# Delta-rule layer: a head's log decays as eight lines in device memory, spread onto a stored mask by an adding transfer

## The chip, the cores and the metric

The kernel runs on one core of one Trainium2 chip, as one launch. The metric is the device time of an execution in microseconds; a kernel's time is the median over its runs. Six units matter here: TensorE (PE, matrix products, with its weight loads as PEld), VectorE (DVE), ScalarE (ACT), GpSimd (POOL), the sync engine (SP, which only issues transfers), and the DMA engines. Each engine works through its own list of instructions in the order laid down when the kernel is built, and waits on semaphores for what others produce.

## What is computed

A bidirectional encoder trunk of two residual layers over 512 tokens of width 1024. Layer 0 mixes the tokens with a gated delta rule, layer 1 with gated linear attention; each is followed by a layer norm, a squared-ReLU feed-forward part and another layer norm. The change lies in layer 0, whose core is, for each of 8 heads and for both directions of time:

```
gc = cumsum(g.reshape(bn, h, n, CHUNK), axis=-1)              # log decays
decay_mat = exp(where(causal, gc[..., :, None] - gc[..., None, :], -inf))
a_mat = where(strict, (kb @ k.T) * decay_mat, 0.0)
sol = triangular_solve(a_mat + I, concat([v * beta, kb * exp(gc)]))
qk = (q @ k.T) * decay_mat
q_dec = q * exp(gc)
for each chunk:                                               # scan
    v_new = u - w @ state
    o = q_dec @ state + qk @ v_new
    state = state * exp(gc_last) + k_dec.T @ v_new
```

Queries and keys are normalized to unit length first. The backward direction is the same on flipped time, and both outputs are added.

## The kernel before

The kernel is written in Python; its loops are unrolled, a scheduler lays out every engine's instructions from the order of the program (earlier lines first, as far as their inputs and buffers are estimated to be free), and allocates buffers from pools by tag. It takes chunks of 128 tokens, so NT = 4 chunks per direction, and 8 chunk problems per head. All products of the projections are made from a high and a low half in three passes (`mm3`, L128 to L130).

`gdn` (L1337) runs the heads as a pipeline written out by hand. In round i it traces `recur` of head i-2 (the scan over chunks), `solve` of head i-1 (the triangular solve by doubling) and `project` of head i (four projections of 512 columns: k, q, v, z, each with a five-tap convolution), then `finish` of head i-2. The scheduler interleaves them, so the projections of one head and, after the last head, the output products (`oa`, the rows of `out_pieces`) stand between the dependent steps of the others.

The steps that the change touches, for head h:

- `GdnConst.masks` (L1170) builds constants on POOL in the setup: a bf16 identity `idb`, a selector `sel` of 6 x 2 x 128 (tag "E" while it is built), two bf16 triangles `mi` holding 0 or -1e30, and masks that the change leaves alone.
- `rows` (L1463), run after the q projection of head h has been convolved and passed through Silu. It squares and sums the transposed k and q, takes logarithms, and forms at L1488 the row sums `rw`: for every token and direction the cumulated log decay less half the logarithm of the key's squared norm. L1490 to L1496 split `rw` into three bf16 parts on DVE; L1499 turns them by four bf16 transposes into the bank `rtp`; L1501 copies the 6 x 512 result to `rt` on ACT. `cj` (L1502) holds the other side's terms per token.
- `solve` (L1519). `kk` (L1528) are the products of the keys. L1532 to L1539: for each direction a matmul with `sel` spreads the rows over all partitions in a PSUM bank `ep` (L1534), its exponential times q gives the query factors `qd` (L1536, L1537). L1547 to L1549 add the triangle to the same bank by a matmul with `idb`. L1553 takes exponentials of the bank, one per chunk, with `cj` as bias, into `E`. `E` times the masked `kk` (L1555) becomes the matrix `ath`, `atl`, from which the inverse is built: `hp` (L1569), `xp` and the copy `Xd` (L1585, L1587), `lv` (L1614) with `pz`, `Dd` and `Xd` in five sizes, and `nw` (L1660, L1661, L1682). L1674 multiplies `E` with the products of keys and queries into `qke`.
- `recur` (L1687): products `m` (L1708) with `vd`, `vn`, `r`, `sn`, then `op` (L1744), the only reader of `qd`.
- `load_z` (L1351) takes a buffer of tag "qd" for one tile of the residual after the last head.

The banks in PSUM are ch 2, pj 3, tp 1, ac 2: `rtp`, `kk` and the transposes of k, q, v use the single bank of tp; `ep`, `hp`, `xp`, `lv`, `nw`, `qk` share the two of ac. Buffers: `E` two tiles of 2 KB per partition (one direction each), `qd` four. `ath`, `atl`, `a4`, `Dd`, `Xd` have one buffer each, so the solves of two heads can't overlap from `ath` on. Weights come through SP into three buffers `wst`, are cast by ACT to `wh` (L102) and completed by DVE as `wl` (L107). Until the layer norm's parameters are fetched after the heads, POOL has only the setup's masks to make. ACT's function tables are changed around each Silu (L1453 and L57).

Of the kernel before, what the change touches and what calls it, by code (L numbers as in the profile page):

```python
# [17 lines left out]
P = 128  # L18
# [1103 lines left out]
class GdnConst:  # L1122


    def __init__(self, c, pool, w_in, w_g, a_log, dt_bias, conv_w, norm_g, x):
        self.c, self.pool = c, pool
        nc = c.nc
        G, V = nc.gpsimd, nc.vector

        M = 4 * A_H  # L1130
        st = c.wst.tile([P, KT, M], F32, name="bst", tag="wst")
        k0 = c.wst.tile([P, KT, P], F32, name="wst", tag="wst")
        c.new_xt()
        c.new_x()

        c.dma(c.xt[0], x[0])
        c.dma(k0, w_in[A_H])
        c.dma(st, w_g)
# [12 lines left out]
        self.ones = pool.tile([P, P], F32, name="ones", tag="vn", bufs=9)  # L1151
        V.memset(self.ones, 1.0)

        self.pz = {}
        for s in (4, 8, 16, 32, 64):
            self.pz[s] = pool.tile([P, 2 * NT, P], F16, name=f"pz{s}", bufs=1)
            V.memset(self.pz[s], 0.0)
        self.gates(st, k0, bia, coef, cw)
        self.ng = pool.tile([P, 1], F32, name="ng", bufs=1)
        nc.sync.dma_start(self.ng, norm_g.unsqueeze(1), allow_slow_non_contiguous=True)  # L1160
        self.masks()
# [8 lines left out]
    def masks(self):  # L1170
        c, pool = self.c, self.pool
        G = c.nc.gpsimd
        self.idb = pool.tile([P, P], BF16, name="idb", bufs=1)
        G.tensor_copy(self.idb, c.ident)
        self.idh = pool.tile([P, P], F16, name="idh", bufs=1)
        G.tensor_copy(self.idh, c.ident)

        sf = pool.tile([6, 2, P], F32, name="self", tag="E", bufs=2)
        G.memset(sf, 0.0)
        for s in range(3):  # L1180
            G.affine_select(out=sf, in_=sf, compare_op=ALU.not_equal, fill=1.0, base=-2 * s,
                            pattern=[[-1, 2], [0, P]], channel_multiplier=1)
        self.sel = pool.tile([6, 2, P], BF16, name="sel", bufs=1)
        G.tensor_copy(self.sel, sf)
        self.mi = [pool.tile([P, P], BF16, name=f"mi{d}", bufs=1) for d in range(2)]
        for d in range(2):
            t = pool.tile([P, P], F32, name="tri", tag="cf", bufs=2)
            self.tri(t, d, False, 0.0, NEG)
            G.tensor_copy(self.mi[d], t)

        self.nd = pool.tile([P, P], F32, name="nd", bufs=1)
        G.tensor_scalar(self.nd, c.ident, -1.0, 1.0, ALU.mult, ALU.add)

        self.same4 = pool.tile([P, P], F16, name="same4", bufs=1)
        self.off = {}
        prev = None
        for w in (4, 8, 16, 32):
            f = pool.tile([P, P], F32, name="blk", tag="cf", bufs=2)
            G.memset(f, 1.0)
            fv = f.rearrange("p (a b) -> p a b", b=w)  # L1200
            G.affine_select(out=fv, in_=fv, compare_op=ALU.is_ge, fill=0.0, base=0,
                            pattern=[[-w, P // w], [0, w]], channel_multiplier=1)
            G.affine_select(out=fv, in_=fv, compare_op=ALU.is_ge, fill=0.0, base=w - 1,
                            pattern=[[w, P // w], [0, w]], channel_multiplier=-1)
            if w == 4:
                G.tensor_copy(self.same4, f)
            else:
                m = pool.tile([P, NT, P], F16, name=f"off{w // 2}", bufs=1)
                G.tensor_tensor(m, f.unsqueeze(1).to_broadcast([P, NT, P]), prev.unsqueeze(1).to_broadcast([P, NT, P]),
                                ALU.subtract)  # L1210
                self.off[w // 2] = m
            prev = f

        ic = pool.tile([P, P // 4, 4], F32, name="ic", tag="cf", bufs=2)
        G.tensor_copy(ic, c.ident.rearrange("p (b c) -> p b c", c=4))
        n = P // 4
        while n > 1:
            n //= 2
            G.tensor_tensor(ic[:, :n, :], ic[:, :n, :], ic[:, n:2 * n, :], ALU.add)
        self.ic = pool.tile([P, 4], F16, name="icc", bufs=1)  # L1220
        G.tensor_copy(self.ic, ic[:, 0, :])
# [115 lines left out]
def gdn(c, w_in, conv_w, a_log, dt_bias, norm_g, w_out, ln_g, ln_b, x, xt, w_next):  # L1337
    tc, nc = c.tc, c.nc
    w_in, w_g = w_in
    with c.banks(ch=2, pj=3, tp=1, ac=2), tc.tile_pool(name="gdn", bufs=1) as pool:  # L1340
        g = GdnConst(c, pool, w_in, w_g, a_log, dt_bias, conv_w, norm_g, xt)
        hi = [c.big.tile([P, 2, S], F32R, name=f"oh{t}", tag=f"xt{t}") for t in range(NT)]
        lo = [pool.tile([P, 2, S], F32R, name="ol", tag="ol", bufs=NT) for t in range(NT)]
        heads = [GdnHead(c, pool, g, h, w_in, hi[h // 2][:, h % 2, :], lo[h // 2][:, h % 2, :]) for h in range(A_H)]
# [6 lines left out]
        def load_z(hf):  # L1351
            if hf:
                tl = pool.tile([P, NT, S], F32, name="z", tag="sil", bufs=3)
            else:
                tl = heads[-1].next.kq
                more = [heads[-1].t2(tag, n).rearrange("p n i -> p (n i)") for tag, n in (("kt", 3), ("qd", 4))]
            for t in range(NT):
                z[t][hf] = tl[:, t, :] if hf or t < 2 else more[t - 2]
                c.dma(z[t][hf], x[t * P:(t + 1) * P, 512 * hf:512 * hf + 512])
# [27 lines left out]
class GdnHead:  # L1387
# [35 lines left out]
    def project(self, done):  # L1423
# [6 lines left out]
        for i, ci in enumerate((A_H + h, h, 2 * A_H + h, 3 * A_H + h)):  # L1430
# [22 lines left out]
                c.exp_ln_after(A.activation(t, t, AF.Silu))  # L1453
            yield 0.69, 0.0
            if i == 1:
                rows = self.rows(done)
                if h:
                    yield from rows
                else:
                    next(rows)  # L1460
                    next(rows)

    def rows(self, done):  # L1463
# [18 lines left out]

        rw = c.small.tile([P, NT, 2], F32, name="rw", tag="rw")
        self.cj = cj = c.small.tile([P, NT, 2], F32, name="cj", tag="cj")
        lnk = lnr[:, 0, :].unsqueeze(2).to_broadcast([P, NT, 2])
        V.scalar_tensor_tensor(rw, lnk, -0.5, g.gc[:, :, :, h], ALU.mult, ALU.add)  # L1488

        rs = c.small.tile([P, NT, 6], BF16, name="rsp", tag="rsp")  # L1490
        r1 = c.small.tile([P, NT, 2], F32, name="r1", tag="r1")
        V.tensor_copy(rs[:, :, 0:2], rw)
        V.tensor_tensor(r1, rw, rs[:, :, 0:2], ALU.subtract)
        V.tensor_copy(rs[:, :, 2:4], r1)
        V.tensor_tensor(r1, r1, rs[:, :, 2:4], ALU.subtract)
        V.tensor_copy(rs[:, :, 4:6], r1)  # L1496
        rtp = self.bank("rtp", BF16, tag="tp")
        for n in range(NT):
            T.transpose(rtp[:6, n, :], rs[:, n, :], g.idb)  # L1499
        self.rt = pool.tile([6, S], BF16, name="rt", tag="rt", bufs=2)  # L1500
        A.copy(self.rt, rtp[:6, :, :].rearrange("p n i -> p (n i)"))  # L1501
        V.scalar_tensor_tensor(cj, lnk, -0.5, g.lg[:, :, :, h], ALU.mult, ALU.add)  # L1502

        pos = c.small.tile([P, NT, 2], F32, name="neg", tag="neg")
# [14 lines left out]
    def solve(self, done):  # L1519
# [8 lines left out]
            T.matmul(kk[:, n, :], self.kc(n), self.kc(n), start=True, stop=True)  # L1528
        yield 0.9, 0.3

        eps, self.qd = [], []
        for d in range(2):  # L1532
            ps = self.bank("ep")
            T.matmul(ps, g.sel[:, d, :], self.rt, start=True, stop=True)  # L1534
            x = self.t2("qd", 4)
            A.activation(x, ps, AF.Exp)  # L1536
            V.tensor_tensor(x, self.kq[:, 1, :].rearrange("p (n i) -> p n i", n=NT), x, ALU.mult)  # L1537
            self.qd.append(x)
            eps.append(ps)  # L1539
        yield 0.63, 1.4  # L1540

        ath, atl = t8("ath", 1), t8("atl", 1)
        kks = self.t2("on", 2)
        V.tensor_tensor(kks, kk, g.nd.unsqueeze(1).to_broadcast([P, NT, P]), ALU.mult)
        a4 = t8("a4", 1)
        ex, ats = [], []
        with c.in_order(mybir.EngineType.PE):  # L1547
            for d in (1, 0):
                T.matmul(eps[d], g.idb, g.mi[d].unsqueeze(1).to_broadcast([P, NT, P]), start=False, stop=True, skip_group_check=True)  # L1549
        for d, ps in enumerate(eps):  # L1550
            e = self.t2("E", 2)
            for n in range(NT):
                A.activation(e[:, n, :], ps[:, n, :], AF.Exp, bias=self.cj[:, n, d:d + 1])  # L1553
            at = kks if d else self.t2("on", 2)
            V.tensor_tensor(at, e, kks, ALU.mult)  # L1555
            us = slice(d * NT, (d + 1) * NT)
# [28 lines left out]
            T.transpose(xp[:, u, :], dd[:, u, :], g.idh)  # L1585
        xd = t8("Xd", 1)
        A.copy(xd, xp)  # L1587

        def half(t, s, i):

# [96 lines left out]
    def recur(self, done):  # L1687
# [51 lines left out]
        self.op = op = self.bank("op", tag="ch")  # L1739
        for n in (1, 2, 0, 3):  # L1740
            mm = [(self.qke[d][:, n, :], vns[d][n]) for d in range(2)]
            mm += [(self.qd[d][:, n, :], states[d][n]) for d in range(2) if states[d][n] is not None]
            for i, (l, r) in enumerate(mm):
                T.matmul(op[:, n, :], l, r, start=i == 0, stop=i == len(mm) - 1)  # L1744
            if n == 2:
# [100 lines left out]
```

## Time and profile before

| | |
|---|---|
| median of 3 runs | 1327.92 us (1327.11 to 1327.92) |
| the profiled execution | 1328.52 us, of which the span from first to last instruction is 1326.6 |
| granted TensorE clock, mean | 0.997 |
| instructions | 22309 |
| DMA | 154.36 MB, 116 GB/s in the mean |
| layer 0's heads, first row sums to last output products | about 42 to 394 us |

The profile has a page (busy shares, 40 slices, queues, the chain of work that ended last, the costliest groups) and views that can be asked for a stretch of time, an engine, a tile or a line of the program. A timeline row reads: start, length, engine, line, operation, tile written <- tiles read, shape, count, and in brackets how long the engine had been idle and what released it. Lengths of matmuls overlap, because they are pipelined, so the time that one takes from PE is read from the distance between starts. A group row reads: line, engine, operation, tiles, count, and the minimum, median and maximum length in ns. A DMA row gives the size and the median time from issue to landing. PE's operations have a line of the helper that issued them, where there is one.

### The profile page before, as it was taken

The page shows a single profiled execution, that of the slowest core. Times are in us where ns is not written, and L with a number is a line of the kernel's source. Part 1 is how long each engine was busy: PE and PEld are TensorE (multiplying, and loading weights), DVE is VectorE, ACT ScalarE, POOL GpSimd, SP SyncE. Part 2 cuts the span into 40 slices and gives each one's busy share as a digit, 9 for nine tenths or more (in the row PEclk, how much of TensorE's full clock was granted, in tenths as well). Part 3 has the DMA queues.
Part 4 walks back from the last instruction along what each step waited for, and adds up shares of the span by engine and source line. Part 5 has one row for each costly group of instructions (what it writes and reads, how often), then busy time and mean ns, then how long its engine had stood idle before and what let it go on. Part 6 is the DMA issues. An engine that isn't in the chain of part 4 may idle for free.

```text
span 1326.6 us, 22309 instructions
## 1 busy us (share of the span) xinstructions
PE 1307.4 (99%) x8659; PEld 1113.2 (84%) x8659; DVE 1107.7 (83%) x1823; ACT 805.2 (61%) x1598; POOL 124.8 (9%) x177
## 2 busy tenths in 40 slices
PE   9999999999999999999999999999999999999996
PEld 7777877787777889999998888888889889999985
DVE  7787888888668988989988787967879789989887
ACT  4757666767643666566667754654456466666656
POOL 5000000000000910101102200000001001101021
PEclk9999999999999999999999999999999999999998
DMA  5210120211222585675648521111216465657465
GB/s 181 96 49 33 49 65 33 64 49 57 73 99 85 189 178 154 156 191 153 151 150 170 149 90 64 65 63 64 95 64 213 105 193 154 149 172 161 142 143 143
DMA packets 44045, 154.36 MB, mean 116 GB/s; under 512 B 5419, under 2 KB 5795, under 8 KB 43939
## 3 DMA queue, kind: packets, MB, share of 16 engines
q1 hardware_dynamic: 32163, 110.85, 24.9%
q0 software_dynamic: 11776, 42.08, 16.1%
q8 instruction: 68, 1.11, 0.3%
q14 instruction: 38, 0.31, 0.1%
HBM read 113.99 MB, written 2.10 MB: 88 GB/s over the span
## 4 chain that ended last, share of the span: by engine, by line
PE 92%; ACT 3%; DVE 3%; issue 1%; DVEq 0%; POOL 0%; ACTq 0%; POOLq 0%
PE fx L128 3%; PE fx L130 3%; PE fx L129 3%; PE pX L130 3%; PE pX L129 3%; PE pX L128 3%; PE pjv L128 3%; PE pjv L129 3%; PE pjv L130 3%; PE m L1708 3%; PE fyz L128 3%; PE fyz L129 3%; PE fyz L130 3%; PE pY L129 2%; PE pY L128 2%; PE pY L130 2%
## 5 line engine op out<-in xcount | busy, mean ns | idle before, releaser
L102 ACT CAST wh<-wst 128x1024 fp32r<-128x1024 f32 x152 | 159.4, 1049 | 110.3 <-PE fyz L129 35.3
L107 DVE TENSOR_TENSOR wl<-wst,wh 128x1024 fp32r<-128x1024 f32 x150 | 184.3, 1229 | 42.2 <-ACT wh L102 41.9
L107 DVE TENSOR_TENSOR w2l<-w2r,w2h 128x1024 fp32r<-128x1024 f32 x92 | 112.3, 1221 | 24.0 <-ACT w2h L102 23.8
L102 ACT CAST w2h<-w2r 128x1024 fp32r<-128x1024 f32 x94 | 98.5, 1048 | 47.4 <-PE pX L130 16.2
L415 POOL DMA_DIRECT2D w2r<-w2r x56 | 48.5, 892 | 493.9 <-DVE w2l L107 247.3
L102 ACT CAST ah<-h 128x1024 fp32r<-128x1024 f32 x56 | 58.9, 1052 | 40.8 <-PE pX L129 18.1
L464 DVE TENSOR_TENSOR wst<-wst 128x512 f32<-128x512 f32 x120 | 79.8, 685 | 0.4
L107 DVE TENSOR_TENSOR al<-h,ah 128x1024 fp32r<-128x1024 f32 x56 | 68.3, 1220 | 5.1 <-ACT ah L102 4.8
L130 PE MATMUL pX<-w2h,al 128*128 128x512 f32 x168 | 66.2, 394 | 0.0
L129 PE MATMUL pX<-w2l,ah 128*128 128x512 f32 x168 | 66.1, 393 | 0.0
L128 PE MATMUL pX<-w2h,ah 128*128 128x512 f32 x168 | 65.8, 392 | 0.0
L128 PE MATMUL pjv<-wh,xth 128*128 128x512 f32 x128 | 54.7, 427 | 0.0
L128 PE MATMUL fx<-xth,wh 128*128 128x256 f32 x192 | 53.6, 279 | 0.0
L130 PE MATMUL fx<-xh,wl 128*128 128x256 f32 x192 | 53.6, 279 | 0.0
L130 PE MATMUL fyz<-xh,wl 128*128 128x256 f32 x192 | 53.6, 279 | 0.0
L128 PE MATMUL fyz<-xh,wh 128*128 128x256 f32 x192 | 53.6, 279 | 0.0
L128 PE MATMUL fx<-xh,wh 128*128 128x256 f32 x192 | 53.5, 278 | 0.0
L129 PE MATMUL fx<-xl,wh 128*128 128x256 f32 x192 | 53.5, 278 | 0.0
L130 PE MATMUL fx<-xth,wl 128*128 128x256 f32 x192 | 53.4, 278 | 0.0
L129 PE MATMUL fx<-xtl,wh 128*128 128x256 f32 x192 | 53.4, 278 | 0.0
L129 PE MATMUL fyz<-xl,wh 128*128 128x256 f32 x192 | 53.4, 278 | 0.0
L129 PE MATMUL pj<-xtl,wh 128*128 128x256 f32 (+1 forms) x160 | 52.0, 326 | 0.2 <-DVE xtl L194 0.2
(538 smaller groups left out, 4320.7 us busy)
## 6 DMA issues: line engine op xcount, KB each, us to landing
wst<-in_w SPq DMA_DIRECT2D x68, 512.0 KB, 4.3
w2r<-in_w SPq DMA_DIRECT2D x60, 512.0 KB, 4.0
w2r<-w2r POOLq DMA_DIRECT2D x56, 512.0 KB, 5.3
wst<-in_a_in SPq DMA_DIRECT2D x32, 512.0 KB, 3.3
wst<-in_b_vr SPq DMA_DIRECT2D x16, 512.0 KB, 3.3
wst<-in_a_out SPq DMA_DIRECT2D x8, 512.0 KB, 3.3
wst<-in_b_in SPq DMA_DIRECT2D x8, 512.0 KB, 3.3
wst<-in_b_out SPq DMA_DIRECT2D x8, 512.0 KB, 3.3
```

Of the source, the lines that this page charges most:

```text
L102: h = nc.scalar.copy(hi, src)
L107: self.halves = h, nc.vector.tensor_tensor(lo, src, hi.bitcast(F32), ALU.subtract)
L128: mm(ps, ah, bh, start=start, stop=False, **kw)
L129: mm(ps, ah, bl, start=False, stop=False, **kw)
L130: self.last_mm = mm(ps, al, bh, start=False, stop=stop, **kw)
L415: nc.gpsimd.dma_start(blocks[a + (q,)], blocks[b + (q,)], accum_op=ALU.add)
L464: plus = lambda a, b: V.tensor_tensor(a, a, b, ALU.add)
L1708: T.matmul(ps[:, d, :], *ops(d), start=True, stop=True)
```

## The change

The row sums are kept in f32 and turned by one transpose into eight lines of 128 (two directions, four chunks). ACT copies them to SBUF and writes them to a tile in device memory. Two transfers from POOL spread these 4 KB over the 128 partitions: one adds them onto a tile `E` that a transfer from SP has filled with the triangles (0 or -1e30, stored once in device memory by the setup), the other writes them plainly to `qd`. The exponentials of `E` then work in place in SBUF, with the same bias as before. The query factors are made from `qd` in place, further down in `solve`, behind the copy of `Xd`. The split, the selector, the bf16 identity, the bf16 triangles and the four matmuls into `ep` are gone. `E` is now one tile for both directions with two buffers of 4 KB per partition, `qd` likewise.

```diff
 def masks(self):
-        self.idb = pool.tile([P, P], BF16, name="idb", bufs=1)
-        G.tensor_copy(self.idb, c.ident)
...
-        sf = pool.tile([6, 2, P], F32, name="self", tag="E", bufs=2)
...
-        self.sel = pool.tile([6, 2, P], BF16, name="sel", bufs=1)
-        G.tensor_copy(self.sel, sf)
-        self.mi = [pool.tile([P, P], BF16, name=f"mi{d}", bufs=1) for d in range(2)]
+        later = pool.tile([P, 2, P], F32, name="later", bufs=1)
         for d in range(2):
-            t = pool.tile([P, P], F32, name="tri", tag="cf", bufs=2)
-            self.tri(t, d, False, 0.0, NEG)
-            G.tensor_copy(self.mi[d], t)
+            self.tri(later[:, d, :], d, False, 0.0, NEG)
+        self.later = self.dram.tile([P, 2, NT, P], F32, name="laterd", bufs=1)
+        for n in range(NT):
+            G.dma_start(self.later[:, :, n, :], later)
...
 def load_z(hf):
-                more = [heads[-1].t2(tag, n).rearrange("p n i -> p (n i)") for tag, n in (("kt", 3), ("qd", 4))]
+                more = [heads[-1].t2("kt", 3).rearrange("p n i -> p (n i)"),
+                        pool.tile([P, 2, S], F32, name="qd", tag="qd", bufs=2)[:, 0, :]]
...
 def project(self, done):
             if i == 1:
+                self.e = pool.tile([P, 2, NT, P], F32, name="E", tag="E", bufs=2)
+                c.nc.sync.dma_start(self.e, g.later)
                 rows = self.rows(done)
...
 def rows(self, done):
-        rw = c.small.tile([P, NT, 2], F32, name="rw", tag="rw")
+        rdn = c.small.tile([P, 2, NT], F32, name="rw", tag="rw")
+        rw = rdn.rearrange("p d n -> p n d")
...
-        V.tensor_copy(rs[:, :, 0:2], rw)
-        V.tensor_tensor(r1, rw, rs[:, :, 0:2], ALU.subtract)
-        V.tensor_copy(rs[:, :, 2:4], r1)
-        V.tensor_tensor(r1, r1, rs[:, :, 2:4], ALU.subtract)
-        V.tensor_copy(rs[:, :, 4:6], r1)
-        rtp = self.bank("rtp", BF16, tag="tp")
-        for n in range(NT):
-            T.transpose(rtp[:6, n, :], rs[:, n, :], g.idb)
-        self.rt = pool.tile([6, S], BF16, name="rt", tag="rt", bufs=2)
-        A.copy(self.rt, rtp[:6, :, :].rearrange("p n i -> p (n i)"))
+        rtp = self.bank("rtp", shape=(2 * NT, P), tag="tp")
+        T.transpose(rtp, rdn.rearrange("p d n -> p (d n)"), c.ident)
+        rt = pool.tile([2 * NT, P], F32, name="rt", tag="rt", bufs=2)
+        A.copy(rt, rtp)
+        row = g.dram.tile([2 * NT, P], F32, name="row", tag="row", bufs=3)
+        self.qd = pool.tile([P, 2, NT, P], F32, name="qd", tag="qd", bufs=2)
+        c.nc.scalar.dma_start(row, rt)
+        every = row.rearrange("u p -> (u p)").partition_broadcast(P)
+        c.nc.gpsimd.dma_start(self.e.rearrange("p d n i -> p (d n i)"), every, accum_op=ALU.add)
+        c.nc.gpsimd.dma_start(self.qd.rearrange("p d n i -> p (d n i)"), every)
...
 def solve(self, done):
-        eps, self.qd = [], []
-        for d in range(2):
-            ps = self.bank("ep")
-            T.matmul(ps, g.sel[:, d, :], self.rt, start=True, stop=True)
-            x = self.t2("qd", 4)
-            A.activation(x, ps, AF.Exp)
-            V.tensor_tensor(x, self.kq[:, 1, :].rearrange("p (n i) -> p n i", n=NT), x, ALU.mult)
-            self.qd.append(x)
-            eps.append(ps)
-        yield 0.63, 1.4
...
-        with c.in_order(mybir.EngineType.PE):
-            for d in (1, 0):
-                T.matmul(eps[d], g.idb, g.mi[d].unsqueeze(1).to_broadcast([P, NT, P]), start=False, stop=True, skip_group_check=True)
-        for d, ps in enumerate(eps):
-            e = self.t2("E", 2)
+        for d in range(2):
+            e = self.e[:, d, :, :]
             for n in range(NT):
-                A.activation(e[:, n, :], ps[:, n, :], AF.Exp, bias=self.cj[:, n, d:d + 1])
+                A.activation(e[:, n, :], e[:, n, :], AF.Exp, bias=self.cj[:, n, d:d + 1])
...
         A.copy(xd, xp)
+        for d in range(2):
+            x = self.qd[:, d, :, :]
+            A.activation(x, x, AF.Exp)
+            V.tensor_tensor(x, self.kq[:, 1, :].rearrange("p (n i) -> p n i", n=NT), x, ALU.mult)
```

`recur` reads `self.qd[:, d, n, :]` in place of `self.qd[d][:, n, :]`, and `GdnConst` is given the pool in device memory.

More of the change, by code (lines that the diff above doesn't have):

```diff
@@ L1122, with __init__ @@
 class GdnConst:
-    def __init__(self, c, pool, w_in, w_g, a_log, dt_bias, conv_w, norm_g, x):
-        self.c, self.pool = c, pool
+    def __init__(self, c, pool, dram, w_in, w_g, a_log, dt_bias, conv_w, norm_g, x):
+        self.c, self.pool, self.dram = c, pool, dram
         nc = c.nc
@@ L1172, in masks @@
         G = c.nc.gpsimd
-        self.idb = pool.tile([P, P], BF16, name="idb", bufs=1)
-        G.tensor_copy(self.idb, c.ident)
         self.idh = pool.tile([P, P], F16, name="idh", bufs=1)
         G.tensor_copy(self.idh, c.ident)
-        sf = pool.tile([6, 2, P], F32, name="self", tag="E", bufs=2)
[L1179 to L1182, printed above, removed]
-        self.sel = pool.tile([6, 2, P], BF16, name="sel", bufs=1)
-        G.tensor_copy(self.sel, sf)
-        self.mi = [pool.tile([P, P], BF16, name=f"mi{d}", bufs=1) for d in range(2)]
+        later = pool.tile([P, 2, P], F32, name="later", bufs=1)
         for d in range(2):
-            t = pool.tile([P, P], F32, name="tri", tag="cf", bufs=2)
-            self.tri(t, d, False, 0.0, NEG)
-            G.tensor_copy(self.mi[d], t)
+            self.tri(later[:, d, :], d, False, 0.0, NEG)
+        self.later = self.dram.tile([P, 2, NT, P], F32, name="laterd", bufs=1)
+        for n in range(NT):
+            G.dma_start(self.later[:, :, n, :], later)
         self.nd = pool.tile([P, P], F32, name="nd", bufs=1)
@@ L1339, in gdn @@
     w_in, w_g = w_in
-    with c.banks(ch=2, pj=3, tp=1, ac=2), tc.tile_pool(name="gdn", bufs=1) as pool:
-        g = GdnConst(c, pool, w_in, w_g, a_log, dt_bias, conv_w, norm_g, xt)
+    with c.banks(ch=2, pj=3, tp=1, ac=2), tc.tile_pool(name="gdn", bufs=1) as pool, \
+            tc.tile_pool(name="gdr", bufs=1, space=bass.MemoryType.DRAM) as dram:
+        g = GdnConst(c, pool, dram, w_in, w_g, a_log, dt_bias, conv_w, norm_g, xt)
         hi = [c.big.tile([P, 2, S], F32R, name=f"oh{t}", tag=f"xt{t}") for t in range(NT)]
@@ L1488, in rows @@
         V.scalar_tensor_tensor(rw, lnk, -0.5, g.gc[:, :, :, h], ALU.mult, ALU.add)
-        rs = c.small.tile([P, NT, 6], BF16, name="rsp", tag="rsp")
-        r1 = c.small.tile([P, NT, 2], F32, name="r1", tag="r1")
-        V.tensor_copy(rs[:, :, 0:2], rw)
-        V.tensor_tensor(r1, rw, rs[:, :, 0:2], ALU.subtract)
-        V.tensor_copy(rs[:, :, 2:4], r1)
-        V.tensor_tensor(r1, r1, rs[:, :, 2:4], ALU.subtract)
-        V.tensor_copy(rs[:, :, 4:6], r1)
-        rtp = self.bank("rtp", BF16, tag="tp")
-        for n in range(NT):
-            T.transpose(rtp[:6, n, :], rs[:, n, :], g.idb)
-        self.rt = pool.tile([6, S], BF16, name="rt", tag="rt", bufs=2)
-        A.copy(self.rt, rtp[:6, :, :].rearrange("p n i -> p (n i)"))
+        rtp = self.bank("rtp", shape=(2 * NT, P), tag="tp")
[8 more added lines that the diff above has]
+        c.nc.gpsimd.dma_start(self.qd.rearrange("p d n i -> p (d n i)"), every)
         V.scalar_tensor_tensor(cj, lnk, -0.5, g.lg[:, :, :, h], ALU.mult, ALU.add)
@@ L1741, in recur @@
             mm = [(self.qke[d][:, n, :], vns[d][n]) for d in range(2)]
-            mm += [(self.qd[d][:, n, :], states[d][n]) for d in range(2) if states[d][n] is not None]
+            mm += [(self.qd[:, d, n, :], states[d][n]) for d in range(2) if states[d][n] is not None]
             for i, (l, r) in enumerate(mm):
```

## Prediction

> **What bounds the kernel now.** I read the page first: the busy shares, then the chain that ended last.
>
> ```profile
> span 1326.6 us, 22309 instructions
> PE 1307.4 (99%) x8659; PEld 1113.2 (84%) x8659; DVE 1107.7 (83%) x1823; ACT 805.2 (61%) x1598; POOL 124.8 (9%) x177
> ...
> PE 92%; ACT 3%; DVE 3%; issue 1%; DVEq 0%; POOL 0%; ACTq 0%; POOLq 0%
> ```
>
> TensorE is the chain in 92% of the span. The change lies in the first layer alone, so next I asked for the busy time in the stretch from the first decay rows to the last head's output products (columns: stretch, length, then busy time of PE, PEld, DVE, ACT, POOL, the granted clock, DMA share, GB/s).
>
> ```profile
> 42.00:394.00 352.00, 348.50 (x3028) 276.04 (x3028) 285.46 (x604) 227.90 (x643) 2.38 (x4) 1.00 0.19 61
> ```
>
> PE lacks 3.5 us of 352, at full clock; DVE has 67 us free, ACT 124, the DMA engines four fifths. Every head's dependent chain is filled with another head's projection, or with output products. So a matmul that disappears should move everything behind it forward, and I price the removed matmuls by the distances between starts in the PE timeline, since the durations there overlap.
>
> **Transpose of the rows (L1499).** Four bf16 transposes become one f32 transpose.
>
> ```profile
> 248.40 0.39 PE L129 MATMUL pjk<-xtl,wh 128*128 128x512 f32 x1
> 248.72 0.39 PE L1499 MATMUL rtp<-idb,rsp 128*6 128x128 bf16 x4
> 249.03 0.50 PE L130 MATMUL pjk<-xth,wl 128*128 128x512 f32 x1
> ...
> 250.03 0.33 PE L1766 MATMUL otp<-ident,fo 128*128 128x128 f32 x1
> 250.19 0.49 PE L1694 MATMUL ktp<-ident,sil 128*128 128x128 f32 x3
> ...
> 48.62 0.39 PE L129 MATMUL pjq<-xtl,wh 128*128 128x512 f32 x1
> 48.85 0.61 PE L1549 MATMUL ep<-mi,idb 128*128 128x512 bf16 x2
> 49.11 0.58 PE L130 MATMUL pjq<-xth,wl 128*128 128x512 f32 x1
> 49.52 0.39 PE L128 MATMUL pjq<-xth,wh 128*128 128x512 f32 x1
> ```
>
> A 512-column projection matmul occupies 0.23 us when nothing interrupts it (48.62 to 48.85). Around the transposes two starts are 0.63 apart (248.40 to 249.03), so the four cost 0.40. One f32 transpose takes 0.16 (250.03 to 250.19). Net 0.24 per head, 1.9 us for eight.
>
> **Mask matmuls (L1549).** In the same rows two projection matmuls and two mask matmuls stand between 48.62 and 49.52: 0.90, less 2 x 0.23, is 0.44 per head, 3.5 us for eight. They go without replacement.
>
> **Spreading matmuls (L1534).** These are found as a pair or interleaved one by one.
>
> ```profile
> 255.89 0.38 PE L1708 MATMUL m<-vt,xf 128*128 128x128 f32 x2
> 256.21 0.39 PE L1534 MATMUL ep<-rt,sel 6*128 6x512 bf16 x1
> 256.52 0.50 PE L128 MATMUL pjk<-xth,wh 128*128 128x512 f32 x1
> 256.86 0.38 PE L1708 MATMUL m<-vt,xf 128*128 128x128 f32 x2
> ...
> 258.42 0.47 PE L128 MATMUL pjq<-xth,wh 128*128 128x512 f32 x1
> 258.73 0.39 PE L129 MATMUL pjq<-xtl,wh 128*128 128x512 f32 x1
> ...
> 341.19 0.60 PE L1534 MATMUL ep<-rt,sel 6*128 6x512 bf16 x2
> 341.72 0.50 PE L129 MATMUL oa<-wl,oh 128*128 128x512 f32 x1
> ...
> 342.29 0.38 PE L1528 MATMUL kk<-sil 128*128 128x128 f32 x2
> 342.51 0.38 PE L1766 MATMUL otp<-ident,fo 128*128 128x128 f32 x2
> ```
>
> As a pair they take 0.53 (341.19 to 341.72). Alone: 255.89 to 256.86 is 0.97; the projection matmul after a change of operand kind keeps 0.31 (258.42 to 258.73) and two f32 products of 128x128 take 0.22 (342.29 to 342.51), so one spreading matmul costs 0.44, two 0.88. Midway is 0.71 per head, 5.7 us for eight. **Removed from PE: 1.9 + 3.5 + 5.7 = 11.1 us**; with pairs everywhere 9.6, with single ones everywhere 12.4.
>
> **Other engines.** DVE loses the five steps of the bf16 split (L1492 to L1496), ACT a copy of 6x512.
>
> ```profile
> L1493 DVE TENSOR_TENSOR r<-rw,rsp x8: 154/157/169, 43.0 to 333.6; 128x8 f32<-128x8 f32 x8
> ...
> L1501 ACT COPY rt<-rtp x8: 570/575/575, 45.1 to 339.5; 6x512 bf16<-6x512 bf16 x8
> ```
>
> Five times 0.16 is 0.8 us of DVE per head, in an engine with free time: nothing in the sum, but it shortens the way to the rows. The copy of 8x128 costs ACT between nothing and the old 0.57. ACT gains one DMA issue per head: no row shows a DMA issued by ACT; a hold of the queue between nothing and a full copy's 0.57 is covered by ACT's 124 free us. The two exponentials and two multiplications of the query factors (L1536, L1537) keep their shapes and only move, from ahead of the decay mask's exponentials to behind the Xd copy (L1587). Their cover is again free time of ACT and DVE; if it were gone they would sit in the solve chain, below 3 us per head. Ahead of E their leaving shortens the chain by as much.
>
> **The new transfers.** Row write on ACT's queue, adding transfer and plain spread on POOL's, mask load on SP's. POOL does nothing else between setup and the final layernorm parameters, so what queues behind its wait for the row is only the spread of the query factors. The adding transfer also waits for the mask load; that waits for E of head h-2 (two buffers), freed at L1674 well before head h has rows. On SP the weight loads stand behind it; they are stopped most of the time for a free buffer already:
>
> ```profile
> SPq L52 <- DVE wl L107: 264.8, 30, 23.7
> ```
>
> That is 264.8 us of the first 420, so I take nothing, at worst a wait of one weight tile. The four setup writes add 0.5 MB and go out beside the first loads or behind them; E is not read before 49.55 (below). I take nothing for them, at worst a microsecond at the start. The price that matters is the **trip from the row sums (rw, L1488) to E**. These are landing times, in the order: the adding transfers of the feed-forward layer (minimum, median, maximum for their line), their group, then a small load and a write to device memory.
>
> ```profile
> DMA to landing us min/median/max: 4.5/5.1/10.3
> ...
> w2r<-w2r POOLq DMA_DIRECT2D x56, 512.0 KB, 5.3
> ...
> out<-xt SPq DMA_DIRECT2D x4, 256.0 KB, 3.5
> ...
> gst<-in_b_gates SPq DMA_DIRECT2D x1, 128.0 KB, 2.1
> ```
>
> The 4 KB write is not in the trace: between 2.1 and 3.5, I take 2.8. The adding transfer is the same size as the group of 56: 5.3. With 0.17 for rw, an estimated 0.5 for the PE transpose to get its turn and at most 0.57 for the copy, the trip is 9.3; with the lowest of each about 7.2, with 10.3 and 3.5 about 15. How long do the heads give it? These are the timeline rows of rw and of the first E exponential in heads 0, 4, 6 and 7:
>
> ```profile
> 42.51 0.17 DVE L1488 SCALAR_TENSOR_TENSOR rw<-lnr,gc 128x8 f32<-128x8 f32 x1
> 49.55 2.24 ACT L1553 ACTIVATE E<-ep,cj 128x128 f32<-128x128 f32 x8 [0.99 <-PE ep L1549]
> ...
> 208.27 0.16 DVE L1488 SCALAR_TENSOR_TENSOR rw<-lnr,gc 128x8 f32<-128x8 f32 x1
> 215.61 1.14 ACT L1553 ACTIVATE E<-ep,cj 128x128 f32<-128x128 f32 x4 [0.95 <-PE ep L1549]
> ...
> 286.63 0.17 DVE L1488 SCALAR_TENSOR_TENSOR rw<-lnr,gc 128x8 f32<-128x8 f32 x1
> 302.89 0.38 ACT L1553 ACTIVATE E<-ep,cj 128x128 f32<-128x128 f32 x1
> ...
> 332.35 0.17 DVE L1488 SCALAR_TENSOR_TENSOR rw<-lnr,gc 128x8 f32<-128x8 f32 x1 [0.57 <-ACT lnr L1481]
> 345.26 0.64 ACT L1553 ACTIVATE E<-ep,cj 128x128 f32<-128x128 f32 x2
> ```
>
> 7.0, 7.3, 16.3 and 12.9 us; the other four heads are like head 6. So a trip of 9.3 is hidden in six heads, where it even ends earlier than E now starts, and is 2.3 and 2.0 late in heads 0 and 4. What stands behind the waiting exponential on ACT are the `vd` and `vn` scalings of the head before and the weight casts, and PE waits for both. But a wait of ACT is not a wait of PE:
>
> ```profile
> 298.71 0.60 ACT L1536 ACTIVATE qd<-ep 128x512 f32<-128x512 f32 x1 [4.45 <-PE ep L1534]
> ```
>
> ACT stood 4.45 us here, while PE in all 352 us missed 3.5. Of the 4.3 us I charge a quarter, 1.1; the ends are 0 and 4.3.
>
> The Trainium skill's DMA: Bandwidth & Descriptors (Anatomy of one DMA) gives a fixed 2.0 us plus bytes/436 GB/s, so 3.2 us for 512 KB; the measured 5.3 speaks against it for an adding transfer. By the page's figures the trip would be about 6.4, inside every head's allowance, and the time 1317.4 on the profiled execution's scale.
>
> **Sum.** -11.1 + 1.1 = -10.0 us. The profiled execution took 1328.5 (span 1326.6), 0.6 above the median of 1327.9, so 1328.5 - 10.0 = 1318.5 for it and **1318** for a median.
>
> **Rivals.**
> *More.* E no longer waits for two PSUM banks nor for PE, so stalls may go too: the whole missing 3.5 us and no charge give 1327.9 - 11.1 - 3.5 = 1313.3. For it: six heads have 3.6 to 7 us of spare. Against: most PE gaps stand before other products.
> *Nothing comes of it, since PE is not the bound.* Weight loads are busy for 276 of 352 us, 78%, matmuls for 99% with modelled ends; if the heads' dependent chain set the pace, PE would only fill more loosely: 1327.9. Against: starts 0.23 apart with no gap. The rule that speaks for it is in the Trainium skill, Perfetto Trace Analysis (Identifying the Most-Contended Engine): matmul busy share is a poor measure of what is left, weight-load share a better one. The rows of starts decide against it here, not the 99%.
> *Slower: the trip is long.* One mechanism in one place: ACT, in order, stands before E in heads 0, 4 and then 7, and PE follows. With the trip of 15 they are late by 8.0, 7.7 and 2.1, together 17.8, less 11.1: +6.7, so 1334.6. It decides from 2 x trip - 14.3 = 11.1, a trip of 12.7. For it: adding transfers have reached 10.3. Against: the median is half of that and this stretch uses 19% of the DMA engines.
> *The change doesn't do what it says:* the query factors fall between the Silu table load and the return to the exponential table, and force reloads.
>
> ```profile
> 275.21 1.28 ACT L1453 ACT_TABLE_LOAD   x1 [5.02 <-DVE sil L1415]
> ```
>
> Two loads of 1.28 for eight heads are 20 us of ACT, within its 124 free; perhaps a third would reach PE, 7 us, giving 1325. Against: by the trip above the spread lands some 15 us after rw, well ahead of the next head's Silu, and ACT had 5.02 us free just ahead of the load.
>
> **Chances.** Forecast (1315 to 1323) 0.55; more 0.10; nothing, or reloads, 0.16; slower 0.19. The instruction order of all engines is laid out anew, which no row can price; that widens the forecast by a few us and puts some of the middle case on either side. The measurement can tell about 0.2% (2.7 us) from no change: faster 0.66, same 0.15, slower 0.19. The range 1312 to 1335 leaves out the deep end of the slower case and little else.
>
> **What would show it.** Right: no `ep` matmuls, about 1.4 us less between the output products of neighbouring heads, PE still lacking under 1% there; rw to landed mask 8 to 11 us; E exponentials starting earlier against the previous head's L1661 products. Wrong: ACT idle before L1553 released by the adding transfer for more than 3 us in several heads and PE idle behind it; more than two table loads per head; PE gaps at the start beside the mask writes; or PE dense and the heads no closer together.

## The result, and the profile after

| | before | after |
|---|---|---|
| median | 1327.92 us | 1341.38 us (1341.09 to 1345.03, 4 runs) |
| ratio to before | | 1.0107, 95% interval 1.0087 to 1.0126 |
| profiled execution: span, mean clock | 1326.6 us, 0.997 | 1343.3 us, 0.989 |

The change makes the kernel 13.5 us slower; 1318 was forecast, with a range that ended at 1335. The profiled execution is the 1345.03 one, so its rows are those of a somewhat longer run than the median.

First the page of the changed kernel (busy time and share of the span, and below it the chain that ended last), then its busy time in the stretch of the heads, which now ends near 415 in place of 394.

```profile
PE 1304.1 (97%) x8603; PEld 1113.6 (83%) x8603; DVE 1106.1 (82%) x1783; ACT 804.4 (60%) x1598; POOL 137.3 (10%) x189
...
PE 79%; ACT 8%; DVE 6%; DMA 5%; issue 1%; DVEq 0%; POOLq 0%; SPq 0%; ACTq 0%
```

```profile
42.00:415.00 373.00, 350.01 (x3003) 281.93 (x3002) 285.90 (x570) 230.49 (x656) 13.46 (x20) 0.98 0.30 89
```

PE has 56 instructions fewer, 7 per head, as intended: no spreading and mask matmuls, one transpose in place of four. But its share of the chain fell from 92% to 79%, with ACT, DVE and DMA in its place, and PE misses 23 us of 373, where it missed 3.5 of 352. The clock column, the share of its full clock that PE was granted, is 0.98, where it was 1.00 before.

The view of waits for 0 to 430 us says what stood (engine, tile and line, released by; total us, times, longest):

```profile
ACT E L1534 <- DMA E<-row: 26.0, 7, 9.0
...
PEld m L1693 <- ACT vd L1708: 16.2, 20, 3.1
...
PE m L1693 <- ACT vd L1708: 10.8, 6, 2.6
...
PE hp L1550 <- DVE a L1539: 5.3, 1, 5.3
```

ACT stood 26.0 us before E, in seven of eight heads, and PE stood behind it: before `m`, whose operand `vd` ACT had not made, and once before `hp`. Two heads show how. Head 2, in the ACT timeline and then the PE timeline:

```profile
138.68 0.62 ACT L1708 ACTIVATE vd<-m,kds 128x128 f32<-128x128 f32 x2
139.20 0.62 ACT L1758 CAST oh<-p 128x512 fp32r<-128x512 f32 x1
139.71 0.45 ACT L1711 ACTIVATE vn<-m 128x128 f32<-128x128 f32 x2
140.03 0.45 ACT L1719 COPY sn<-m 128x128 f32<-128x128 f32 x2
143.51 2.44 ACT L1534 ACTIVATE E<-E,cj 128x128 f32<-128x128 f32 x8 [3.03 <-DMA E<-row]
145.86 0.60 ACT L1708 ACTIVATE vd<-m,kds 128x128 f32<-128x128 f32 x2
```

```profile
142.07 0.60 PE L1693 MATMUL m<-r,xf 128*128 128x128 f32 x4
...
143.21 0.40 PE L130 MATMUL pjq<-xth,wl 128*128 128x512 f32 x1
146.26 0.74 PE L1693 MATMUL m<-vd,kt 128*128 128x128 f32 x4 [2.65 <-ACT vd L1708]
```

In ACT's order the eight exponentials of head 2's E stand between the first and the second step of head 1's scan. They wait 3.03 us for the transfer; `vd` of the second step, whose input `m` PE had made at 142.07, comes behind them, and the next `m` on PE waits for that `vd`. PE's own order holds it there: it takes up the projection products behind `m` (from 146.75) only after it. That these could have run earlier was not tried.

Head 0 (row sums, issue of the row write, issue of the adding transfer, E; then PE):

```profile
44.81 0.17 DVE L1485 SCALAR_TENSOR_TENSOR rw<-lnr,gc 128x8 f32<-128x8 f32 x1
```

```profile
46.10 0.54 ACTq L1493 DMA_DIRECT2D row<-rt  x1
...
57.39 2.15 ACT L1534 ACTIVATE E<-E,cj 128x128 f32<-128x128 f32 x7 [9.02 <-DMA E<-row]
```

```profile
49.74 0.94 POOL L1495 DMA_DIRECT2D E<-row  x1 [20.17 <-DMA row<-rt]
```

```profile
57.07 0.39 PE L128 MATMUL pjv<-xth,wh 128*128 128x512 f32 x1
62.78 0.37 PE L1550 MATMUL hp<-icc,a 128*128 128x4 f16 x8 [5.32 <-DVE a L1539]
...
63.58 0.63 PE L130 MATMUL pjv<-xth,wl 128*128 128x512 f32 x1
64.01 0.63 PE L128 MATMUL pjv<-xth,wh 128*128 128x512 f32 x1
...
68.27 0.63 PE L130 MATMUL pjz<-xth,wl 128*128 128x512 f32 x1
68.70 0.58 PE L128 MATMUL pjz<-xth,wh 128*128 128x512 f32 x1
69.12 0.40 PE L129 MATMUL pjz<-xtl,wh 128*128 128x512 f32 x1
69.36 0.40 PE L130 MATMUL pjz<-xth,wl 128*128 128x512 f32 x1
```

The trip from the row sums to E took 12.6 us: 1.3 to the issue of the write, 3.6 until POOL saw the row, 7.7 until E could be read. In all eight heads, from `rw` to the first E exponential, it was 8.1 to 12.6, with a median near 10.2. PE reached `hp` in its order 5.3 us early. Behind that gap the projection products start 0.43 us apart (63.58 to 64.01, 68.27 to 68.70), where 0.24 is the rule (69.12 to 69.36): for 6 us PE ran at half its clock (granted 0.50 from 62.28 to 69.11).

Against the kernel before, the first output products `op` of heads 0, 1 and 2 come 8.6, 14.2 and 17.3 us later, those of head 7 18.8 later: the loss arises in the first three heads. From then on the lag stays between 16 and 19 us, so the 1.4 us that each head was to gain do not show either.

### The profile page after: what moved, and what is told of

The parts are those of the page before. It is cut to its first block, busy times and chain, and to the rows that moved or that the text cites. A ratio compares the mean times of both kernels' runs of the same rounds, so it can differ in the third digit from the quotient of the medians.

```text
span 1343.3 us, 22245 instructions
## 1 busy us (share of the span) xinstructions
PE 1304.1 (97%) x8603; PEld 1113.6 (83%) x8603; DVE 1106.1 (82%) x1783; ACT 804.4 (60%) x1598; POOL 137.3 (10%) x189
## 3 DMA queue, kind: packets, MB, share of 16 engines
HBM read 126.57 MB, written 2.65 MB: 96 GB/s over the span
## 4 chain that ended last, share of the span: by engine, by line
PE 79%; ACT 8%; DVE 6%; DMA 5%; issue 1%; DVEq 0%; POOLq 0%; SPq 0%; ACTq 0%
PE fx L128 3%; PE fx L130 3%; PE pX L129 3%; PE pX L130 3%; DMA E<-row 3%; PE fx L129 3%; PE pX L128 3%; PE pjv L129 3%; PE pjv L128 3%; PE pjv L130 3%; PE m L1693 3%; PE fyz L130 3%; PE fyz L128 3%; PE fyz L129 2%; PE pY L129 2%; PE pY L130 2%
```

## Experiments

**Theories.** *A*: the removed PE work is worth its price, but the readers of the transferred rows are laid into the order of ACT (and `hp` into that of PE) ahead of the landing; the engines stand there in order, and PE pays again with the clock. *B*: the trip is part of the heads' dependent chain, whatever the order. *C*: the transfers and the setup's writes cost time by themselves. *D*: the removed PE work is worth nothing. Four runs were to tell these apart.

**Without the adding transfer.** The decays are missing from E; its exponentials read the bare mask.

```diff
-        c.nc.gpsimd.dma_start(self.e..., every, accum_op=ALU.add)
-                A.activation(e[:, n, :], e[:, n, :], AF.Exp, bias=self.cj[:, n, d:d + 1])
+                A.activation(e[:, n, :], e[:, n, :], AF.Exp, bias=c.bias[-12.0])
```

> The adding transfer is left out; row write, plain spread, mask load and setup writes stay, and E's exponentials work on the bare mask with a constant bias (the decays are missing from E). Theory A (ACT and PE stand in their own order before E and its product hp until the transfer lands, and the removed 11.1 us of PE work is real): E waits for nothing, so 1317 to 1321. Theory C (the transfers and the setup writes cost time by themselves): 1335 or more. Theory D (removed PE work is worth nothing, the dependent chain sets the pace): 1326 to 1330.

Measured: 1334.31 (1332.37 to 1336.6), ratio 1.0047 (1.0032 to 1.0062). No theory had it. The ACT and PE timelines of head 6 in this kernel tell why:

```profile
304.22 1.15 ACT L1570 ACTIVATE qd<-qd 128x512 f32<-128x512 f32 x2 [2.52 <-DMA qd<-row]
```

```profile
306.78 0.75 PE L1692 MATMUL m<-vd,kt 128*128 128x128 f32 x4 [2.40 <-ACT vd L1707]
```

The reader of the other spread, the query factors' exponential, now stands in the same place: 10.9 us of ACT waits for `qd<-row` in all. So the edit removed one of two such waits, and did not separate A from C.

**No transfers at all.** The decays are missing from E and from the query factors; both read a constant mask in SBUF.

```diff
-        c.nc.scalar.dma_start(row, rt)
-        c.nc.gpsimd.dma_start(self.e..., every, accum_op=ALU.add)
-        c.nc.gpsimd.dma_start(self.qd..., every)
-                c.nc.sync.dma_start(self.e, g.later)
+                A.activation(e[:, n, :], g.mask[:, d, :], AF.Exp, bias=c.bias[-12.0])
+            A.activation(x, g.later[:, d, :, :], AF.Exp)
```

> No transfers at all for the decays: no row write, no spreads, no mask load, no setup writes; the exponentials of E and of the query factors read the constant mask in SBUF (the decays are missing from both). The matmuls that the change removed stay removed. Theory A: the removed 11.1 us of PE work show in full, 1315 to 1319. Theory D: 1326 to 1329, as before the change.

Measured: 1316.12 (1315.79 to 1316.45), ratio 0.9909 (0.9894 to 0.9924), 11.8 below the kernel before. D falls. As E is also free of every wait here, the gain could have come from that; so PE work was put back into this kernel, with no reader:

```diff
+        for d in range(2):
+            ps = self.bank("ep")
+            for i in range(2):
+                T.matmul(ps, g.idb, g.idb.unsqueeze(1).to_broadcast([P, NT, P]), start=i == 0, stop=i == 1)
```

> The kernel without transfers (1316.1) with PE work of the removed kind put back and nothing waiting for it: per head four bf16 products of 128x128 by 128x512 into two banks that nobody reads. If PE is the bound where the change lies, each costs what the starts in the trace of before show, 0.22 in a pair: 32 x 0.22 = 7.0, 1323.1 (1322 to 1326 with some taken singly at up to 0.44). If the 1316 came from E no longer having to wait for its inputs rather than from less PE work: 1316 to 1319.

Measured: 1322.85 (1321.49 to 1323.09), 6.7 more against 7.0 expected. Here PE work counts at the distance of its starts, although nothing depends on it.

**Mask from SBUF.** No mask in device memory, no setup writes.

```diff
-        self.later = self.dram.tile([P, 2, NT, P], F32, name="laterd", bufs=1)
-        for n in range(NT):
-            G.dma_start(self.later[:, :, n, :], later)
+        self.later = later.unsqueeze(2).to_broadcast([P, 2, NT, P])
-                c.nc.sync.dma_start(self.e, g.later)
+                for d in range(2):
+                    c.nc.sync.dma_start(self.e[:, d, :, :], g.later[:, d, :, :])
```

> The mask is filled from a tile in SBUF by two SP transfers per head; the mask in device memory and its four setup writes are gone. If the setup writes delayed the first weights and so all that follows: about 2.3 us less than the changed kernel, 1339 (the lag of the first row sums). If head 0's stand absorbs it or the writes are harmless: 1341 to 1342.

Measured: 1339.54 (1338.02 to 1344.16), ratio 1.0091 (1.0071 to 1.0112), so 1.8 less, an interval that overlaps the changed kernel's. The stretch 0 to 42 us (PE, PEld, DVE, ACT, POOL, clock, DMA share, GB/s) supports it, in the changed kernel and in this one:

```profile
0.00:42.00 42.00, 38.59 (x183) 30.50 (x184) 29.76 (x60) 21.64 (x34) 18.86 (x43) 0.96 0.56 193
```

```profile
0.00:42.00 42.00, 39.94 (x199) 32.51 (x200) 31.92 (x69) 24.12 (x47) 13.68 (x39) 1.00 0.55 186
```

In the changed kernel the second weight tile is on the chain, as the chain of its first 30 us shows (start, length, what):

```profile
8.40 10.43 DMA wst<-in_a_in
```

Its four setup writes of 128 KB are issued between 3.45 and 6.5 us, and the tile issued at 8.40 lands 10.4 us later; the row sums come at 44.81 in place of 42.51, and with the mask in SBUF at 41.40.

**E held in heads 1 to 7.** The exponentials of E and of the query factors are queued on ACT behind the second scan step's `vn` of the head before. Nothing else changes.

```diff
-                A.mul(vn, m2[:, d, :], -1.0 if step else 1.0)
+                i = A.mul(vn, m2[:, d, :], -1.0 if step else 1.0)
+                if step == 1 and d:
+                    self.next.hold = i
...
+            with c.tc.issue_after(self.hold.ins) if h else contextlib.nullcontext():
                 for n in range(NT):
                     A.activation(e[:, n, :], e[:, n, :], AF.Exp, bias=self.cj[:, n, d:d + 1])
```

> In heads 1 to 7 the exponentials of E, and those of the query factors, are held on ACT behind the second step's vn of the head before. Theory A: the stands of heads 1 to 7 before E go (6.1 + 3.0 + smaller ones), the lag that heads 1 and 2 added between output products (5.6 + 3.1) comes back, at least half of it: 1331 to 1336; head 0's 9 us stand stays. Theory B (the trip's length itself is in the solve chain, whatever the order): E only gets later, 1341 or more.

Measured: 1326.54 (1325.59 to 1328.56), ratio 0.9991 (0.9981 to 1.0): 14.8 back, more than A's 1331 to 1336 allowed for, and the transfers are as they were. B and C fall as main causes. The waits of this kernel, and its head 2 in the ACT timeline:

```profile
ACT E L1535 <- DMA E<-row: 7.4, 1, 7.4
```

```profile
135.83 0.63 ACT L1710 ACTIVATE vd<-m,kds 128x128 f32<-128x128 f32 x2 [2.24 <-PE m L1695]
136.34 0.44 ACT L1713 ACTIVATE vn<-m 128x128 f32<-128x128 f32 x2
136.66 2.45 ACT L1535 ACTIVATE E<-E,cj 128x128 f32<-128x128 f32 x8
```

E now runs without a wait, 14.9 us behind its row sums (121.81), later by this measure than the 10.6 of the changed kernel, and the kernel is faster: the trip's length was not the price, the place of its reader was. The one wait left is head 0's. How much of the 14.8 is owed to the held query factors, and not to E, was not separated.

The control puts the same hold of E (heads 1 to 7) into the kernel before:

> A control: the kernel before, with the E exponentials of heads 1 to 7 held behind the same vn of the head before. Its E waits for PSUM and PE, not for a transfer. Theory A: nothing to gain, 1327 to 1331. Rival: the hold would help any kernel (vd and vn ahead of E shorten the scan), so what the held run gave back says nothing of the transfer: 1313 to 1322.

Measured: 1330.47 (1329.73 to 1331.17), ratio 1.0019 (1.001 to 1.0028): it costs that kernel 2.8 us. Of these two kernels the hold helps only the one whose E awaits a transfer.

**Head 0.** Its E waits behind head 1's q convolution; to have that traced in time, head 1's first two projections come ahead of the rest of head 0's solve. First alone, then together with the hold of heads 1 to 7.

```diff
+            if i == 1:
+                for gen, n in ((s, 2), (p, 16)):
+                    for _ in range(n):
+                        next(gen)
...
+            with contextlib.nullcontext() if h else c.tc.issue_after(g.scaled.ins):
                 for n in range(NT):
                     A.activation(e[:, n, :], e[:, n, :], AF.Exp, bias=self.cj[:, n, d:d + 1])
```

> Only head 0: its E exponentials are held on ACT behind the next head's q convolution scaling (the k and q projections of head 1 are traced ahead of the rest of head 0's solve), so that the first hp product is laid later on PE; heads 1 to 7 as in the changed kernel. Theory A: PE's 5.3 us gap at 57 us and the half-clock stretch behind it (about 12 projection products at 0.43 in place of 0.23, 2.5 us) go, heads 1 and 2 still stand (5.6 + 3.1 us of lag): 1333 to 1337. If head 0's stand is absorbed later: 1340 to 1342.

Measured: 1336.84 (1334.44 to 1339.83), 4.5 below the changed kernel, as A expected. The hold and the earlier place of the projections were not separated.

> The hold of heads 1 to 7 and that of head 0 together; all transfers as in the changed kernel. Theory A: the held kernel's 1326.5 less PE's remaining 3.7 us gap before hp in head 0 and about 2 us of half clock behind it: 1319 to 1322. If what is left is the transfers themselves: 1325 to 1327.

Measured: 1324.14 (1321.95 to 1326.63), ratio 0.9971 (0.9959 to 0.9982): 2.4 of the 4.5 to 7.5 expected. A part of what is missing shows in the setup of the profiled run: this run's stretch of 0 to 42 us, and then that of the run below, which has the mask in SBUF too:

```profile
0.00:42.00 42.00, 37.42 (x170) 29.95 (x170) 26.08 (x54) 19.83 (x29) 18.54 (x43) 0.92 0.57 193
```

```profile
0.00:42.00 42.00, 39.94 (x197) 32.81 (x198) 31.72 (x68) 23.74 (x44) 13.71 (x39) 1.00 0.55 183
```

PE misses 2.5 us more of the setup with the mask in device memory, at a clock of 0.92. The kernel with heads 1 to 7 held, from which the sum started, has the same setup writes, but in its profile PE is busy for 39.70 us of this stretch at clock 1.00, and head 0's row sums come at 43.26, against 47.43 here. Why the same writes cost more in one profile than in the other is not shown.

> Both holds, and the mask from SBUF without device memory and setup writes. The setup share adds to the holds: 1.8 us below the run with both holds, 1317 to 1320. If the setup delay only mattered while head 0 stood: the same as both holds.

Measured: 1320.87 (1319.01 to 1323.27), ratio 0.9939 (0.9922 to 0.9955): 3.3 below the run with both holds, where 1.8 was expected. With all three it is 6.8 us below the kernel before, and the fastest that computes the whole; the two below are level with it.

**The last head, and an earlier hold.** Two edits of this version: head 7 not held; and that, with the hold behind the first step's `vn`.

> Both holds and the SBUF mask, but head 7 not held: in the run with all of them the last head's output products came 44 us after head 6's (36 in the kernel before), with PE missing 3 us at 400 to 440 us. If the hold of the last head, which has no later projection to cover it, is what is left against the 1316 without transfers: 1316 to 1319. If not: 1320 to 1323.

Measured: 1320.68 (1317.73 to 1321.58). A miss: the last head's hold is not what is left.

> As the run without head 7's hold, but heads 1 to 6 are held behind the first step's vn in place of the second's, some 3 us earlier. Theory A says that only a place ahead of the landing costs: the rows had about 4 us between landing and exponential with the later hold, so no stand comes back and the time is within 2 us of that run. If a landing runs late in a head: 3 us or more above it.

Measured: 1321.53 (1320.93 to 1323.49), within 2 us, as A said.

**The query factors back ahead of E.** One part of the change undone, its transfers kept.

```diff
         yield 0.9, 0.3
+        for d in range(2):
+            x = self.qd[:, d, :, :]
+            A.activation(x, x, AF.Exp)
+            V.tensor_tensor(x, self.kq[:, 1, :].rearrange("p (n i) -> p n i", n=NT), x, ALU.mult)
```

> One part of the change undone: the query factors are traced ahead of E again, as before the change; the transfers stay. On ACT they then stand among the first E exponentials and wait for the second spread, which lands after the first. Theory A: a later stand on ACT, so longer gaps on PE, 1343 to 1350. If the place of the factors is indifferent: 1340 to 1343. If the later place was itself the loss: 1336 or less.

Measured: 1348.6 (1345.79 to 1350.1), ratio 1.0154 (1.0139 to 1.0169), 7.2 slower than the changed kernel. The waits of this kernel:

```profile
ACT E L1538 <- DMA E<-row: 30.5, 7, 7.9
...
PE m L1693 <- ACT vd L1708: 12.8, 6, 3.7
...
ACT qd L1527 <- DMA qd<-row: 4.0, 2, 2.2
```

The later place of the query factors is a part of the change that pays, given the transfers.

**The account**, from the medians, each step against the one above:

| | us | step |
|---|---|---|
| before | 1327.9 | |
| no transfers, decays missing (removed PE work, no wait before E) | 1316.1 | -11.8 |
| transfers, readers held, mask from SBUF | 1320.9 | +4.8 |
| the same with the mask in device memory | 1324.1 | +3.3 |
| head 0 not held | 1326.5 | +2.4 |
| heads 1 to 7 not held: the change | 1341.4 | +14.8 |

The kernel before, measured beside these runs, stayed at medians of 1327.6 to 1327.9. The two smaller steps, 3.3 and 2.4, lie between kernels whose runs overlap, so their sizes are rough.

What makes up the 4.8 was not separated. Head 0 still has a short gap before `hp` in these kernels (0.8 to 2.3 us). And in the profiled run with all three, at 1323.27 the slowest of its four, DVE stood for a transfer in the same way, before the residual that `load_z` fetches into a buffer of tag "qd":

```profile
357.86 0.69 DVE L311 SCALAR_TENSOR_TENSOR qd<-qd,oa 128x512 f32<-128x512 f32 x1 [3.01 <-DMA qd<-in_x]
```

Behind it stood head 7's `Dd`, for which PE waited 2.54 us before an `lv`; 3.4 us at a granted clock of 0.50 followed.

## Why the prediction was wrong, step by step

- *PE is the bound, and removed matmuls count at the distance of their starts: 11.1 us.* Right: 11.8 without transfers, where E has no wait either, and 6.7 of 7.0 when work was put back. The rival *nothing comes of it* falls, and with it the reading of the Trainium skill's Perfetto Trace Analysis (Identifying the Most-Contended Engine) that gave it a chance.
- *The trip is 9.3 us (7.2 to 15).* A median of 10.2, and 12.6 in head 0: a fair estimate with head 0 too short. The 6.4 by the Trainium skill's DMA: Bandwidth & Descriptors (Anatomy of one DMA) was reached in no head (8.1 is the shortest); the adding transfer alone has a median of 6.0 from issue to landing, against the 3.2 of its formula.
- *The heads give it 7.0, 7.3, 12.9 and five times some 16 us.* **This step failed.** These were distances between the row sums and E in an order laid out for matmuls, and they did not carry over. The measured trips (12.6, 9.9, 10.6, 8.1, 10.5, 8.4, 9.3, 10.9) set against them would be late in heads 0 and 4 alone, by 8.8 us; ACT really stood in seven heads, for 26.0. What changed is the room between the rows and their reader. In heads 1, 2 and 3 of the kernel before, `rw` comes 26.8, 26.8 and 27.2 us ahead of the first `op` of the head before, and E 10.1, 10.6 and 10.9 ahead of it. After the change the rows come only 22.8, 22.2 and 19.1 ahead of that `op`, and E, after ACT's wait, 13.0, 11.6 and 10.9. In the new order ACT stood ready for E 3.6, 3.7, 7.6, 6.5 and 7.5 us behind the row sums in heads 0 to 4, and 8.1 and 8.9 behind them in heads 6 and 7 (the trip less ACT's wait, by its timeline), where the old order had given 7.0, 16.7, 16.2, 16.3 and 7.3, and 16.3 and 12.9. Why the order put the rows later was not tried. That it would be laid out anew was written down, and priced at "a few us".
- *A wait of ACT is not a wait of PE: a quarter is charged.* Failed too. Holding the readers recovered 17.2 us (1341.38 to 1324.14) for 26.0 us of ACT waits, two thirds; PE's own waits for `vd` and before `hp` were 10.8 and 5.3. The 4.45 us wait it leaned on was one wait, of which PE felt little; here PE's `m` waited six times for a `vd` that ACT had not made, and the clock was not in the sum.
- *The setup writes cost nothing, at worst 1 us.* Mis-sized: 1.8 by itself, 3.3 beside the holds, both between medians of runs that overlap.
- *The query factors move at no cost.* Right in sign: their later place is worth 7.2. No table loads were added; there are still two per head.
- *The rival "the trip is long"* named the mechanism (ACT in order before E, PE behind it) but tied it to a trip of over 12.7 and to heads 0, 4 and 7, by the same allowances. It came with shorter trips, in heads 0, 1, 2 and 4 above all. Its sign showed in the profile as the prediction said: ACT idle before E for over 3 us in several heads, with PE idle behind.

## What to carry to other kernels

When an input moves from a computed tile to a transfer, the room that the old order left for it is no allowance: ask where the reader will be laid once its old inputs are gone, and which other work stands behind it in that engine's order. Where a transfer's landing is later than the order assumes, queue its readers explicitly behind work that needs nothing from it; that was worth 15 us here, more than the removed matmuls. And an idle PE is to be priced with the slow stretch that can follow the gap.

## What the runs showed of the hardware

The clock was dearer than expected. The kernel before has no gap of 0.7 us or more on PE among its heads, and a granted clock of 1.00 there. In the changed kernel the gaps of 5.32, 2.11, 2.65 and 2.49 us were each followed by projection products 0.42 to 0.57 apart (0.23 to 0.32 otherwise), at a granted clock of 0.50, for 3.4 us, and for 6.8 after the longest; those of 0.80, 0.85, 0.86 and 1.80 us by none. The Trainium skill, TensorE: Matmul & The Clock Gate (HAM oscillation — how this bites in real kernels), advises against idle gaps over about 3.4 us; by these rows gaps of 2.1 to 2.7 us were enough.

But the length of a gap does not decide alone. In the setup of the changed kernel a gap of 1.12 us, with one of 0.52 close behind, was followed by 3.4 us at half the clock too; and in the run with the query factors ahead of E, PE stood 3.23 us before 177.01 at no such price. The half-clock stretches of a trace lie multiples of 3.41 us apart, so the idle time can be counted in cells of that grid (columns as above). Two cells at the 2.65 us gap of the changed kernel:

```profile
144.20:147.61 3.41, 1.35 (x8) 1.07 (x9) 1.96 (x5) 3.41 (x13) 0.00 (x0) 1.00 0.18 73
147.61:151.02 3.41, 3.41 (x21) 2.73 (x21) 2.10 (x7) 1.82 (x4) 0.00 (x0) 0.50 0.00 0
```

Three at the 3.23 us gap of the other run:

```profile
171.88:175.29 3.41, 1.90 (x9) 1.19 (x7) 0.88 (x4) 0.16 (x1) 0.00 (x0) 1.00 0.99 286
175.29:178.70 3.41, 1.69 (x11) 1.53 (x12) 0.48 (x1) 3.41 (x12) 0.00 (x0) 1.00 0.58 237
178.70:182.11 3.41, 3.41 (x19) 2.52 (x18) 3.17 (x7) 3.41 (x13) 0.00 (x0) 1.00 0.00 0
```

The first gap leaves PE idle for 2.06 us of one cell, and the next runs at half the clock. The second falls across the edge of two cells, 1.51 and 1.72 us, and the clock stays. From 10 to 430 us of all the traces here, every cell with 1.73 us or more of idle PE was followed by half the clock; of those with 1.2 to 1.72, some were and more were not.

The kernels with the new transfers also scatter more. The four to ten runs of each spread over 2.6 to 6.1 us, where the two kernels without transfers spread over 0.7 and 1.6 and the kernel before, in 15 runs, over 1.8.
